# Last output projection's first operands in places of long dead tiles, two stores by GpSimd's queue, splits in pairs, and HGRN's sum in two F32R passes

## The chip, the cores and the metric

The kernel runs on one core of a Trainium2 chip. The metric is the device time of one execution in microseconds; a kernel's time is the median of its runs.

## The reference

One decoder layer on x (1, 2048, 1024) in float32:

```python
h = rmsnorm(x, norm1_w)
proj = h @ w_in                                  # HGRN2 columns | RWKV-7 columns
o_hg = hgrn2(...)                                # 4 heads of 128
o_rw = rwkv7(...)                                # 8 heads of 64
x = x + concat([o_hg, o_rw], -1) @ w_out         # the output projection
x = x + conv_ffn(rmsnorm(x, norm2_w), ...)       # up, causal conv of width 3, silu gate, down; 2816 wide
return rmsnorm(x, final_norm_w)

# the end of hgrn2, per head of 128 channels
o = o * rsqrt(mean(o * o, axis=-1) + 1e-6)
o = o * norm_w * silu(g_raw)
```

## The kernel before

The 2048 tokens are cut into four blocks of 512 (NBLK = 4, BLK = 512). Activations are held with channels on the 128 partitions and tokens in the free dimension.

Large products use no fp32 matmul. Each operand is split into a rounded F32R part and an F32R rest: `hi` is a copy by ACT, `lo` is the difference by DVE (`split_to`, L241 to L243, and `split`, L245 to L251). A product is then three matmuls of 512 columns, hi·hi, hi·lo and lo·hi (`mm3`, L264 to L267), that add up in one PSUM bank.

Phase 1 holds three generators. `dense` issues input projections, and from `out_block` also the output projections of the blocks 0 to 2, into the bank `pj`. `rw_stream` steps through RWKV and `hg_stream` through HGRN. A loop calls one step of each stream and then issues about 2.0 us of dense matmuls by its own count (TICK), so that PE has dense work while a step's other engines are busy. A `yield` is the end of a step.

One `hg_unit` is one head in one block, 16 in all. Its end is what the change touches: the attention output `op` in PSUM is squared by ACT into `osq` (L1044, one step), summed over the 128 channels by a matmul with `ones`, an fp32 matrix of ones (L1047, next step), and turned to a factor by Ln and Exp; DVE multiplies it in, and a DMA stores the result to `oT`. RWKV's sums do the same with `group`, in two passes over a split square (`parts`, then `add_up`, L1057 to L1059).

`out_block(2, ...)` is the last dense work of phase 1. For two halves of its tokens (`i2`) and two halves of the 1024 outputs (`dh`) it multiplies `oT` by `w_out` (tiles `wh`, `wl`, `hh`, `hl`), adds x (`xh`, L408) and stores to `x1d` by SP's queue (L410). RWKV's last value `yo` of the last block is stored to `oT` by GpSimd's queue (L928).

The output projection of block 3 follows in the pool `op`. It runs over dh (2) and over k, the eight groups of 128 channels, in the order 0, 1, 4, 5, 2, 3, 6, 7. Each step loads and splits 128x512 of `w_out` (to `woh`, `wol`) and, for dh = 0, of `oT` (`Bh`, `Bl`, held in `ohl[k]`), and issues twelve matmuls into four banks `wacc`. The first three raw tiles of either kind lie in six places `uraw`, the later ones in `Bh[2]` and `Bl[2]`; they are loaded by SP's queue in the order in which they are written down (L1171). In each of the big tiles `Bh` and `Bl` a list index says which of several places is used.

Where a tile is allocated in a place that an earlier tile held, its first writer waits for the earlier tile's last reader or writer, and also for its stores. The instructions of each engine, and of each DMA queue, go in order; that order is set by a scheduler from the order in the code and its own estimate of times, so an edit of tiles moves instructions.

Of the kernel before, what the change touches and what calls it, by code (L numbers as in the profile page):

```python
# [7 lines left out]
F32 = mybir.dt.float32  # L8
F32R = mybir.dt.float32r
BF16 = mybir.dt.bfloat16  # L10
U32 = mybir.dt.uint32
AF = mybir.ActivationFunctionType
# [6 lines left out]
P = 128  # L19
# [45 lines left out]
def tile_layer(ctx, tc, consts, x, norm1_w, w_in, hg_lb_logits, hg_norm_w, rw_shift_mu, rw_w0, rw_w2,  # L65
# [34 lines left out]
        V.memset(t_, v)  # L100
        return t_

    ones = cp.tile([P, P], F32, name="ones")
    V.memset(ones, 1.0)
    eps6 = eps_tile(1e-6, "eps6")
    epsgn = eps_tile(64e-5, "epsgn")

# [131 lines left out]
        return b11, b22, b12, b21  # L239

    def split_to(hi, lo, src):  # L241
        S.copy(hi, src)
        V.tensor_sub(lo, src, hi.bitcast(F32))  # L243

    def split(pool, src, shape, name, bufs):  # L245

# [16 lines left out]
    def mm3(acc, lhs, rhs, first, last, skip=False):  # L263
        (lh, ll), (rh, rl) = lhs, rhs  # L264
        TE.matmul(acc, lh, rh, start=first, stop=False, skip_group_check=skip)  # L265
        TE.matmul(acc, lh, rl, start=False, stop=False, skip_group_check=skip)  # L266
        TE.matmul(acc, ll, rh, start=False, stop=last, skip_group_check=skip)  # L267

    def phase1(c1):
# [15 lines left out]
        Af = hp.tile([P, 4, P], F32, name="Af")  # L285
        for t_ in (TTs, Af):
            nc.gpsimd.memset(t_, 0.0)
        group = hp.tile([P, P], F32R, name="group")
        hh = hp.tile([P, KD, BLK], F32R, name="hh")
        hl = hp.tile([P, KD, BLK], F32R, name="hl")  # L290

# [82 lines left out]
        def out_block(nb, oh=None, ol=None, then=None):  # L374


            for i2 in range(2):
                for dh in range(2):
                    accs = [bank("pj") for _ in range(2)]
                    for k in range(KD):  # L380
                        if i2 == 0 and dh == 0 and oh is None:
                            raw = stg("sg", "oraw", 2)
                            dma(raw, oT[nb][k * P:(k + 1) * P, :])
                            split_to(hh[:, k, :], hl[:, k, :], raw)
                        if i2 == 1 and dh == 0 and oh is not None:
                            raw = stg("sg", "oraw", 2)[:, 0:256]
                            dma(raw, oT[nb][k * P:(k + 1) * P, 256:512])
                            split_to(hh[:, k, 256:512], hl[:, k, 256:512], raw)
                        raw = wp.tile([P, 512], F32, tag="wraw", name="woraw", bufs=4)
                        wload(raw, w_out[0, k * P:(k + 1) * P, dh * 512:dh * 512 + 512])  # L390
                        wh, wl = split(wp, raw, [P, 512], "w", 4)
                        if k == KD - 2:
                            inputs = dh == 0 and (i2 == 0) == (oh is None)
                            xh = [wp.tile([P, BLK], F32, tag="wraw", name="xh", bufs=4) if inputs else
                                  stg("sg", "xh", 2) for _ in range(2)]
                            for q in range(2):
                                t0 = nb * BLK + (i2 * 2 + q) * P
                                dma(xh[q], x[0, t0:t0 + P, dh * 512:dh * 512 + 512])
                        for q in range(2):
                            is_ = slice((i2 * 2 + q) * P, (i2 * 2 + q + 1) * P)  # L400
                            lhs = ((hh[:, k, is_], hl[:, k, is_]) if oh is None or i2 == 1 else
                                   (oh[k // 4][:, k % 4, is_], ol[k // 4][:, k % 4, is_]))
                            mm3(accs[q], lhs, (wh, wl), k == 0, k == KD - 1)
                            if i2 == 1 and dh == 1 and q == 1:
                                next_block(then, k)
                            yield 680
                    for q in range(2):
                        V.tensor_add(xh[q], accs[q], xh[q])  # L408
                        r0 = (i2 * 2 + q) * P
                        dma(x1d[nb][r0:r0 + P, dh * 512:dh * 512 + 512], xh[q])  # L410

        rows = {}

# [77 lines left out]
        def constants():  # L491

            dma(w2a2[0:64, :], rw_w2[0])
            dma(w2a2[64:128, :], rw_a2[0])
            dma(cst, consts[:, 0:C_ID])
            S.copy(group, blk1)
            dma(g2, rw_g2[0])

        def spread():
# [433 lines left out]
        def hg_unit(nb, j):  # L933
# [108 lines left out]
                TE.matmul(op[:, ts_], SH[:, b, :], q[:, ts_], start=False, stop=True)  # L1042
            sq = rp.tile([P, BLK], F32, tag="hk", name="osq")
            act(sq, op, AF.Square)  # L1044
            yield
            ms = bank("hg")
            TE.matmul(ms, ones, sq, start=True, stop=True)  # L1047
            act(sq, ms, AF.Ln, bias=eps6, scale=1.0 / 128)
            act(sq, sq, AF.Exp, scale=-0.5)
            yield  # L1050
# [68 lines left out]
    with ExitStack() as c2:  # L1119
# [34 lines left out]


        with tc.tile_pool(name="op", bufs=1, reuse_waits="tile") as op_:
            crow = [op_.tile([88, P], F32, name=f"crow{i}") for i in range(2)]
            def rows_of_conv():
                load(crow[0], conv_w[0, 0:2, :].rearrange("w (k p) -> (w k) p", p=P))
                load(crow[1][0:44, :], conv_w[0, 2:3, :].rearrange("w (k p) -> (w k) p", p=P))  # L1160
                load(crow[1][44:88, :], conv_b.rearrange("w (k p) -> (w k) p", p=P))

            b = NBLK - 1
            for _ in range(2):
                pst("skip")
            ohl = {}
            order = [None]

            def load(t_, src):

                i_ = dma(t_, src)  # L1171
                if order[0] is not None:
                    tc.add_manual_dep(i_.ins, order[0].ins.name, NOSYNC, reason="order of loads")
                order[0] = i_

            loader[0] = load
            rings = {"o": (Bh[2], []), "w": (Bl[2], [])}

            def ring(nm, src):

                t_, n_ = rings[nm]
                if len(n_) < 3:
                    v = wr.tile([P, 4, P], F32, tag="uraw", name="uraw", bufs=6).rearrange("p k c -> p (k c)")
                else:
                    v = t_[:, len(n_) % 4, :]
                n_.append(0)
                load(v, src)
                return v

            def take(k):  # L1190

                raw = ring("o", oT[b][k * P:(k + 1) * P, :])
                ohl[k] = tuple(t_[3 + 2 * (k // 4)][:, k % 4, :] for t_ in (Bh, Bl))
                split_to(*ohl[k], raw)

            def weights(k, dh):
                raw = ring("w", w_out[0, k * P:(k + 1) * P, dh * 512:dh * 512 + 512])
                wh, wl = (op_.tile([P, 512], F32R, tag="wo" + c, name="wo" + c, bufs=3) for c in "hl")
                split_to(wh, wl, raw)
                return wh, wl  # L1200

            xt = {}

            def x_tile(i):
                xt[i] = op_.tile([P, 512], F32, tag="xh", name="xh", bufs=8)

            for i in range(4):
                x_tile(i)
            for dh in range(2):
                accs = [pst("wacc") for _ in range(4)]  # L1210
                for n, k in enumerate((0, 1, 4, 5, 2, 3, 6, 7)):
                    w = weights(k, dh)
                    if dh == 0:
                        take(k)
                    if n == 5:
                        for i in range(4):
                            t0 = b * BLK + i * P
                            if dh:
                                x_tile(i)
                            load(xt[i], x[0, t0:t0 + P, dh * 512:dh * 512 + 512])  # L1220
                    if dh == 0 and n == 6:
                        rows_of_conv()
                    if dh == 1 and n == 4:
                        for i, (lo_, hi_) in enumerate(((0, 88), (88, 176))):
                            vps = pst("cps")
                            TE.transpose(vps[:, 0:88], crow[i], ident[0:88, 0:88])
                            V.tensor_copy(cvt[:, lo_:hi_], vps[:, 0:88])
                        A0 = up_raw(0)
                    if dh == 1 and 2 <= n:
                        for j in range(2):  # L1230
                            q = 2 * (n - 2) + j
                            build(0, (0, 1, 4)[q // 4], q % 4)
                    for i in range(4):
                        is_ = slice(i * P, (i + 1) * P)
                        mm3(accs[i], (ohl[k][0][:, is_], ohl[k][1][:, is_]), w, n == 0, n == KD - 1)
                for i in range(4):
                    V.tensor_add(xt[i], accs[i], xt[i])
                    dma(x1d[b][i * P:(i + 1) * P, dh * 512:dh * 512 + 512], xt[i])
# [350 lines left out]
```

## Time and profile before

| | us |
|---|---|
| median of 3 runs | 2686.07 |
| lowest and highest run | 2683.67, 2687.13 |
| the profiled execution's own time | 2685.16 |
| its span in the trace | 2683.4 |
| PE busy in it | 2596.0 |
| DVE busy | 1952.4 |
| ACT busy | 1359.4 |

The mean clock granted to TensorE was 0.992 of full speed. A row of a timeline reads: start in us, busy us, engine, line, operation, output<-inputs, shapes, count of joined instructions, and in brackets the idle time before it with what ended it. Phase 1 ends near 1343 us; the projection of block 3 begins at 1351.01; the last span to 2683 belongs to the ConvFFN.

### The profile page before, as it was taken

To read this page: it belongs to the slowest core of one execution; us is meant where nothing else is said; L and a number is where in the kernel's file an instruction comes from. 1 tells how busy PE (TensorE), PEld (TensorE's weight loads), DVE (VectorE), ACT (ScalarE), POOL (GpSimd) and SP (SyncE) were. 2 spreads that over 40 slices of the span, in tenths; PEclk is the share of its full clock that TensorE was granted. 3 is DMA by queue.
4 is the path that set the end of the run, shared out by engine and by line. 5 is a ranking of instruction groups with operands and counts; after the bars stand their busy time and mean duration, and the time that the engine had idled before them with its cause. 6 is when DMAs were issued, how large, how long until landed. Compare 5 with 4: busy or idle time off the path is not lost.

```text
span 2683.4 us, 47889 instructions
## 1 busy us (share of the span) xinstructions
PE 2596.0 (97%) x18059; PEld 2089.4 (78%) x18059; DVE 1952.4 (73%) x3729; ACT 1359.4 (51%) x2183; POOL 381.7 (14%) x684
## 2 busy tenths in 40 slices
PE   7999999999999999999989999999999999999998
PEld 5877777777777777777778888887888887788887
DVE  4877667576576765767668789988998888676556
ACT  5555453544634545344447665456555545445444
POOL 6433222212322122222100000000000000000000
PEclk9999999999999999999999999999999999999999
DMA  8645443355643556734484458756754463898665
GB/s 302 205 162 169 162 134 123 119 161 200 208 131 119 162 189 200 259 122 131 157 273 146 135 183 264 246 172 206 252 199 146 153 200 122 313 323 281 203 193 185
DMA packets 312830, 510.54 MB, mean 190 GB/s; under 512 B 46879, under 2 KB 143509, under 8 KB 312597
## 3 DMA queue, kind: packets, MB, share of 16 engines
q1 hardware_dynamic: 258225, 329.65, 37.3%
q0 software_dynamic: 54304, 177.80, 20.3%
q8 instruction: 142, 2.33, 0.4%
q14 instruction: 91, 0.75, 0.1%
q10 hardware_dynamic: 68, 0.02, 0.0%
HBM read 373.13 MB, written 134.22 MB: 189 GB/s over the span
## 4 chain that ended last, share of the span: by engine, by line
PE 68%; DVE 10%; DMA 7%; issue 6%; ACT 6%; POOL 1%; SPq 0%; DVEq 0%; POOLq 0%; ACTq 0%
PE pj L265 7%; PE pj L266 7%; PE pj L267 6%; PE ua L265 4%; PE ua L267 4%; PE ua L266 4%; PE da L266 2%; PE da L267 2%; PE da L265 2%; PE ud L266 2%; PE ud L267 2%; PE ud L265 2%; PE hg L979 2%; PE db L267 2%; PE db L265 2%
## 5 line engine op out<-in xcount | busy, mean ns | idle before, releaser
L265 PE MATMUL pj<-hh,wh 128*128 128x512 f32 x960 | 398.0, 415 | 6.2 <-ACT rkv L120 2.9
L266 PE MATMUL pj<-hl,wh 128*128 128x512 f32 x960 | 377.4, 393 | 0.0
L267 PE MATMUL pj<-hh,wl 128*128 128x512 f32 x960 | 377.0, 393 | 0.0
L265 PE MATMUL ua<-Bh,uwh 128*128 128x512 f32 x704 | 276.4, 393 | 3.6 <-ACT m L120 2.5
L267 PE MATMUL ua<-Bh,uwl 128*128 128x512 f32 x704 | 274.3, 390 | 0.0
L266 PE MATMUL ua<-Bl,uwh 128*128 128x512 f32 x704 | 274.1, 389 | 0.0
L265 PEld LDWEIGHTS pj<-hh,wh 128*128 128x128 f32 x960 | 181.0, 189 | 57.9 <-issue 9.0
L267 PEld LDWEIGHTS pj<-hh,wl 128*128 128x128 f32 x960 | 180.9, 188 | 40.0 <-issue 0.6
L266 PEld LDWEIGHTS pj<-hl,wh 128*128 128x128 f32 x960 | 181.3, 189 | 35.9 <-issue 2.6
L249 ACT CAST uwh<-uraw 128x512 fp32r<-128x512 f32 x220 | 134.6, 617 | 129.9 <-PE ua L266 56.2
L250 DVE TENSOR_TENSOR dal<-draw,dah 128x512 fp32r<-128x512 f32 x138 | 95.1, 689 | 111.9 <-ACT dah L249 111.7
L250 DVE TENSOR_TENSOR uwl<-uraw,uwh 128x512 fp32r<-128x512 f32 x220 | 147.1, 684 | 35.2 <-ACT uwh L249 35.2
L249 ACT CAST dah<-draw 128x512 fp32r<-128x512 f32 x138 | 85.8, 622 | 166.1 <-PE da L266 79.6
L265 PEld LDWEIGHTS ua<-Bh,uwh 128*128 128x128 f32 x704 | 132.2, 188 | 34.2 <-ACT m L120 6.0
L267 PEld LDWEIGHTS ua<-Bh,uwl 128*128 128x128 f32 x704 | 132.2, 188 | 28.0 <-DVE uwl L250 0.4
L266 PEld LDWEIGHTS ua<-Bl,uwh 128*128 128x128 f32 x704 | 132.2, 188 | 26.6
L265 PE MATMUL ud<-Bh,uwh 128*128 128x512 f32 x352 | 138.0, 392 | 0.0
L267 PE MATMUL ud<-Bh,uwl 128*128 128x512 f32 x352 | 137.0, 389 | 0.0
L266 PE MATMUL ud<-Bl,uwh 128*128 128x512 f32 x352 | 137.0, 389 | 0.0
L1459 POOL DMA_DIRECT2D gd<-y x2 | 1.1, 555 | 952.3 <-DVE y L1457 952.3
L266 PE MATMUL da<-dbl,dah 128*128 128x512 f32 x332 | 129.5, 390 | 1.0 <-DVE dbl L250 1.0
L267 PE MATMUL da<-dbh,dal 128*128 128x512 f32 x332 | 129.2, 389 | 0.0
(575 smaller groups left out, 6245.0 us busy)
## 6 DMA issues: line engine op xcount, KB each, us to landing
uraw<-in_w_up_dram SPq DMA_DIRECT2D x176, 256.0 KB, 3.3
woraw<-in_w_out_dram POOLq DMA_DIRECT2D x96, 256.0 KB, 3.5
br<-gd SPq DMA_DIRECT2D x88, 256.0 KB, 4.2
draw<-Sg SPq DMA_DIRECT2D x88, 256.0 KB, 3.6
draw<-Tw SPq DMA_DIRECT2D x88, 256.0 KB, 3.4
gd<-y SPq DMA_DIRECT2D x86, 256.0 KB, 2.8
Sg<-br SPq DMA_DIRECT2D x72, 256.0 KB, 2.6
xt<-x1d SPq DMA_DIRECT2D x32, 512.0 KB, 5.9
```

Source lines behind the costliest of these rows:

```text
L249: S.copy(hi, src)
L250: V.tensor_sub(lo, src, hi.bitcast(F32))
L265: TE.matmul(acc, lh, rh, start=first, stop=False, skip_group_check=skip)
L266: TE.matmul(acc, lh, rl, start=False, stop=False, skip_group_check=skip)
L267: TE.matmul(acc, ll, rh, start=False, stop=last, skip_group_check=skip)
L979: TE.matmul(o, kt[:, t0:t0 + 64], qs, start=True, stop=True, tile_position=(0, e * 64))
L1459: (dma if end is None else nc.gpsimd.dma_start)(gd_[2 * h + b][fb * P:(fb + 1) * P, :], ys[0][:, b * BLK:(b + 1) * BLK])
```

## The change

It has six parts.

- The matrix `ones` becomes an F32R tile of the phase's pool, written by ACT (Identity with scale 0 and bias 1 over `blk1`).
- HGRN's squares are split into `hi` and `lo` in the step of the Square, in places of `Sf` and `VT`; two F32R matmuls (`add_up`) replace the fp32 matmul.
- The last two stores of `out_block(2)` (second half of the tokens, dh = 1) go to GpSimd's queue.
- The first pair `woh`, `wol` is allocated at the opening of the pool, ahead of everything else there; the x tiles are allocated when they are loaded. `ohl` uses the places 5 for k < 4 and 3 for k of 4 and more, the other way round than before.
- The splits of the first steps are tied in the order of the code: woh, Bh, woh, Bh on ACT, and wol, Bl, wol, Bl on DVE.
- The first k step issues four hi·hi, then four hi·lo, then four lo·hi, in place of three per row block.

Lines 265 to 267 become 263 to 265, L408 becomes L406, and the matmuls of the last projection have L1247.

```diff
-    ones = cp.tile([P, P], F32, name="ones")
-    V.memset(ones, 1.0)
...
     def split_to(hi, lo, src):
-        S.copy(hi, src)
-        V.tensor_sub(lo, src, hi.bitcast(F32))
+        c_ = S.copy(hi, src)
+        return c_, V.tensor_sub(lo, src, hi.bitcast(F32))
...
-        group = hp.tile([P, P], F32R, name="group")
+        group, ones = (hp.tile([P, P], F32R, name=nm) for nm in ("group", "ones"))
...
-                        dma(x1d[nb][r0:r0 + P, dh * 512:dh * 512 + 512], xh[q])
+                        (nc.gpsimd.dma_start if nb == NBLK - 2 and i2 and dh else dma)(
+                            x1d[nb][r0:r0 + P, dh * 512:dh * 512 + 512], xh[q])
...
             S.copy(group, blk1)
+            act(ones, blk1, AF.Identity, bias=1.0, scale=0.0)
...
             act(sq, op, AF.Square)
+            hi, lo = (rp.tile([P, BLK], F32R, tag=tag, name="part") for tag in ("Sf", "VT"))
+            split_to(hi, lo, sq)
             yield
             ms = bank("hg")
-            TE.matmul(ms, ones, sq, start=True, stop=True)
+            add_up(ms, ones, hi, lo)
...
         with tc.tile_pool(name="op", bufs=1, reuse_waits="tile") as op_:
+            wo_ = {c: [op_.tile([P, 512], F32R, tag="wo" + c, name="wo" + c, bufs=3)] for c in "hl"}
...
+            split_done = []
+
+            def split_next(hi, lo, raw):
+                pair = split_to(hi, lo, raw)
+                if 0 < len(split_done) < 6:
+                    for i_, o_ in zip(pair, split_done[-1]):
+                        tc.add_manual_dep(i_.ins, o_.ins.name, NOSYNC, reason="order of splits")
+                split_done.append(pair)
+
             def take(k):
 
                 raw = ring("o", oT[b][k * P:(k + 1) * P, :])
-                ohl[k] = tuple(t_[3 + 2 * (k // 4)][:, k % 4, :] for t_ in (Bh, Bl))
-                split_to(*ohl[k], raw)
+                ohl[k] = tuple(t_[5 - 2 * (k // 4)][:, k % 4, :] for t_ in (Bh, Bl))
+                split_next(*ohl[k], raw)
 
             def weights(k, dh):
                 raw = ring("w", w_out[0, k * P:(k + 1) * P, dh * 512:dh * 512 + 512])
-                wh, wl = (op_.tile([P, 512], F32R, tag="wo" + c, name="wo" + c, bufs=3) for c in "hl")
-                split_to(wh, wl, raw)
+                wh, wl = (wo_[c].pop() if wo_[c] else
+                          op_.tile([P, 512], F32R, tag="wo" + c, name="wo" + c, bufs=3) for c in "hl")
+                split_next(wh, wl, raw)
                 return wh, wl
...
-            for i in range(4):
-                x_tile(i)
...
-                            if dh:
-                                x_tile(i)
+                            x_tile(i)
                             load(xt[i], x[0, t0:t0 + P, dh * 512:dh * 512 + 512])
...
-                    for i in range(4):
-                        is_ = slice(i * P, (i + 1) * P)
-                        mm3(accs[i], (ohl[k][0][:, is_], ohl[k][1][:, is_]), w, n == 0, n == KD - 1)
+                    terms = [(ohl[k][0], w[0]), (ohl[k][0], w[1]), (ohl[k][1], w[0])]
+                    first = n == 0 and dh == 0
+                    for q in range(12):
+                        i, t_ = (q % 4, q // 4) if first else (q // 3, q % 3)
+                        TE.matmul(accs[i], terms[t_][0][:, i * P:(i + 1) * P], terms[t_][1],
+                                  start=n == 0 and t_ == 0, stop=n == KD - 1 and t_ == 2)
```

The order of instructions, ACT at the end of phase 1 and the start of the last projection, before: `wh` are the last weights of `out_block(2)`, `yo` is RWKV's last value, `woh` and `Bh` belong to the last projection, and the number behind a name tells one place from another.

```order
L249 CAST wh<-woraw 128x512 x2
L120 ACTIVATE yo<-yo,vt 128x512 x2
L116 ACT_TABLE_LOAD
L242 CAST woh<-uraw 128x512 x3
L242 CAST Bh_14735<-uraw 128x512 x2
L242 CAST Bh_14738<-uraw 128x512
L242 CAST Bh_14738<-Bh_14730 128x512
```

The same place now.

```order
L247 CAST wh<-woraw 128x512 x2
L118 ACTIVATE yo<-yo,vt 128x512 x2
L247 CAST wh<-woraw 128x512 x2
L114 ACT_TABLE_LOAD
L240 CAST woh<-uraw 128x512
L240 CAST Bh_14818<-uraw 128x512
L240 CAST woh<-uraw 128x512
L240 CAST Bh_14818<-uraw 128x512
L240 CAST woh<-uraw 128x512
L240 CAST Bh_14815<-uraw 128x512
```

The casts of woh and Bh alternate, and two casts of `wh` moved behind those of `yo`.

DVE at the same place, before: `wl` are the rests of the weights of `out_block(2)`, L927 writes `yo`, L408 adds x.

```order
L1052 TENSOR_TENSOR osq<-osq,hgg 128x512
L926 TENSOR_TENSOR yo<-yo,BV 128x1024
L250 TENSOR_TENSOR wl<-woraw,wh 128x512
L927 TENSOR_TENSOR yo<-rw,yo 128x1024
L408 TENSOR_TENSOR xh<-pj,xh 128x512 x2
L243 TENSOR_TENSOR wol<-uraw,woh 128x512 x3
L243 TENSOR_TENSOR Bl_14736<-uraw,Bh_14735 128x512 x2
L243 TENSOR_TENSOR Bl_14739<-uraw,Bh_14738 128x512
```

And now.

```order
L1054 TENSOR_TENSOR osq<-osq,hgg 128x512
L926 TENSOR_TENSOR yo<-yo,BV 128x1024
L248 TENSOR_TENSOR wl<-woraw,wh 128x512
L927 TENSOR_TENSOR yo<-rw,yo 128x1024
L248 TENSOR_TENSOR wl<-woraw,wh 128x512 x2
L406 TENSOR_TENSOR xh<-pj,xh 128x512 x2
L241 TENSOR_TENSOR wol<-uraw,woh 128x512
L241 TENSOR_TENSOR Bl_14819<-uraw,Bh_14818 128x512
L241 TENSOR_TENSOR wol<-uraw,woh 128x512
L241 TENSOR_TENSOR Bl_14819<-uraw,Bh_14818 128x512
L241 TENSOR_TENSOR wol<-uraw,woh 128x512
L241 TENSOR_TENSOR Bl_14816<-uraw,Bh_14815 128x512
```

Two subtractions `wl` now stand behind L927, where none stood, and wol and Bl alternate; the Bl of the third pair (place 14816) is the one for k = 4.

PE at the first k step of the projection, before.

```order
L267 MATMUL pj<-wh,hl 128x512
L265 MATMUL wacc<-woh,Bh_14735 128x512
L266 MATMUL wacc<-wol,Bh_14735 128x512
L267 MATMUL wacc<-woh,Bl_14736 128x512
L265 MATMUL wacc<-woh,Bh_14735 128x512
L266 MATMUL wacc<-wol,Bh_14735 128x512
```

And now.

```order
L265 MATMUL pj<-wh,hl 128x512
L1247 MATMUL wacc<-woh,Bh_14818 128x512 x4
L1247 MATMUL wacc<-wol,Bh_14818 128x512 x4
L1247 MATMUL wacc<-woh,Bl_14819 128x512 x4
L1247 MATMUL wacc<-woh,Bh_14818 128x512
L1247 MATMUL wacc<-wol,Bh_14818 128x512
```

The first four matmuls need woh and Bh alone; wol is read by the fifth, where it was by the second, and Bl by the ninth, where it was by the third.

## The prediction

> **What bounds the kernel now.** I read the page's busy times first, then the chain of waits, then windows around the edit, then the timeline of each engine there.
>
> ```profile
> PE 2596.0 (97%) x18059; PEld 2089.4 (78%) x18059; DVE 1952.4 (73%) x3729; ACT 1359.4 (51%) x2183; POOL 381.7 (14%) x684
> PE 68%; DVE 10%; DMA 7%; issue 6%; ACT 6%; POOL 1%; SPq 0%; DVEq 0%; POOLq 0%; ACTq 0%
> 25.00:1300.00 1275.00, 1233.57 (x11970) 972.21 (x11968) 859.29 (x2048) 615.14 (x976) 344.07 (x614) 0.99 0.52 168
> 1300.00:1343.00 43.00, 38.40 (x267) 29.44 (x264) 26.10 (x54) 19.89 (x34) 5.92 (x11) 0.92 0.55 177
> 1343.00:1356.00 13.00, 5.12 (x13) 3.73 (x13) 5.87 (x10) 4.26 (x8) 0.72 (x1) 0.61 0.91 312
> 1356.00:1368.00 12.00, 12.00 (x54) 9.91 (x53) 4.78 (x8) 4.67 (x8) 0.00 (x0) 1.00 0.41 136
> 1368.00:1416.00 48.00, 46.60 (x205) 37.59 (x204) 38.72 (x67) 28.54 (x49) 0.00 (x0) 1.00 0.94 312
> ```
>
> TensorE is busy 97% of the span, so time is won in two ways only: fewer microseconds of matmul, or a hole closed. After the span, the columns of a window are the busy times of PE, weight load, DVE, ACT and POOL, then granted clock, DMA share and GB/s. The worst hole is 1343 to 1356, between the mixers and the last output projection: PE works 5.12 of 13 us, at a clock of 0.61. From 1356 to 1368 PE is full and the DMA engines are half idle (0.41); from 1368 to 1416 they are nearly full (0.94).
>
> The timelines of PE, ACT, DVE and SP show how the hole arises, with two pieces of the chain of waits:
>
> ```profile
> 1342.73 0.40 PE L267 MATMUL pj<-wh,hl 128*128 128x512 f32 x1
> 1351.01 0.80 PE L265 MATMUL wacc<-woh,Bh 128*128 128x512 f32 x1 [7.88 <-ACT Bh L242]
> 1352.58 0.63 PE L265 MATMUL wacc<-woh,Bh 128*128 128x512 f32 x1
> 1353.00 0.63 PE L266 MATMUL wacc<-wol,Bh 128*128 128x512 f32 x1
> 1356.03 0.40 PE L265 MATMUL wacc<-woh,Bh 128*128 128x512 f32 x1
> 1356.26 0.39 PE L266 MATMUL wacc<-wol,Bh 128*128 128x512 f32 x1
> 1339.80 1.28 ACT L116 ACT_TABLE_LOAD   x1
> 1348.78 1.66 ACT L242 CAST woh<-uraw 128x512 fp32r<-128x512 f32 x3 [7.70 <-DMA oT<-yo]
> 1350.35 1.66 ACT L242 CAST Bh<-uraw 128x512 fp32r<-128x512 f32 x3
> 1340.96 0.68 DVE L250 TENSOR_TENSOR wl<-woraw,wh 128x512 fp32r<-128x512 f32 x1
> 1341.56 1.22 DVE L927 TENSOR_TENSOR yo<-rw,yo 128x1024 f32<-128x1024 f32 x1
> 1342.69 1.28 DVE L408 TENSOR_TENSOR xh<-pj,xh 128x512 f32<-128x512 f32 x2
> 1325.95 18.36 SPq L410 DMA_DIRECT2D x1d<-xh  x4
> 1344.36 0.46 SPq L1171 DMA_DIRECT2D Bl<-in_w_out_dram  x1
> 1341.56 1.23 DVE yo L927
> 1343.34 5.34 DMA oT<-yo
> ```
>
> The last matmul of the mixers starts at 1342.73. The first of the projection wants Bh. ACT was free at 1341.1 (the table load's end), yet did the three woh casts at 1348.78 and Bh behind them: their tiles stand where `yo` stood, and `yo` is released by its store, 5.34 us long. So the hole is a wait for a place; the first operands had been loaded long before. When PE resumes it goes at a pitch of 0.42 us (1352.58 to 1353.00), not 0.23 (1356.03 to 1356.26). The first k step, 12 matmuls, takes 1351.01 to 1356.03 = 5.02 us where 12 x 0.23 = 2.7 would do.
>
> **The change part by part.** *The HGRN sum* (16 units). Rows of the PE timeline, fp32 sum of HGRN, then the two-pass sums RWKV uses; then the groups:
>
> ```profile
> 138.25 1.02 PE L1047 MATMUL hg<-osq,ones 128*128 128x512 f32 x2
> 138.70 0.79 PE L265 MATMUL pj<-hh,wh 128*128 128x512 f32 x1
> 139.33 0.39 PE L266 MATMUL pj<-hl,wh 128*128 128x512 f32 x1
> 1331.62 0.39 PE L1058 MATMUL rw<-part,group 128*128 128x512 f32 x1
> 1332.08 0.39 PE L1058 MATMUL rw<-part,group 128*128 128x512 f32 x1
> 136.37 0.60 ACT L120 ACTIVATE osq<-hg 128x512 f32<-128x512 f32 x1 [3.36 <-PE hg L1042]
> L1059 PE MATMUL rw<-part,group 128*128 128x512 f32 x48 | 20.1, 419 | 3.1 <-DVE part L243 3.1
> L1058 PE MATMUL rw<-part,group 128*128 128x512 f32 x48 | 20.0, 416 | 1.5 <-ACT part L242 1.5
> L1047 PE MATMUL hg<-osq,ones 128*128 128x512 f32 x32 | 16.5, 596 | 0.0
> L243 DVE TENSOR_TENSOR part<-yo,part 128x1024 fp32r<-128x1024 f32 x8 | 9.8, 1222 | 13.3 <-ACT part L242 13.3
> ```
>
> The fp32 pair pushes the next matmuls back until 139.33; less one pj pitch of 0.23 it costs 139.33 - 0.23 - 138.25 = 0.85 us. Two F32R passes cost 1332.08 - 1331.62 = 0.46. Saved: 0.39 x 16 = 6.2 us of PE.
>
> Against it stand one cast and one subtraction per unit, and PE now waits for them. A cast costs a third of the woh group, 0.55 us; a subtraction 0.68 alone (the wl row), 0.60 in a queue (1341.56 - 1340.96). From the Square's start the second pass needs 0.60 + 0.55 + 0.60 = 1.75 us, the first 1.15. In the row shown the sum came 138.25 - 136.37 = 1.88 us after the Square's start, filled with dense matmuls. That covers it by 0.13 us, if neither ACT nor DVE is busy elsewhere; DVE is so 859.29/1275 = 67% of this stretch. The nearest price is RWKV's: its splits are twice as wide (a subtraction 1.22), its two passes are laid out alike, and the groups show 3.1 + 1.5 = 4.6 us of waits over 24 pairs of sums, 0.19 each. Bounds: 0 (fully covered, as L1047 is now) to the whole added 1.15 us per unit, 0 to 18.4. I take RWKV's 0.19 x 16 = 3.0, because shape and order are its own. The 8.8 us of added casts and 9.6 of subtractions lie on engines with room, and cost nothing besides while PE has matmuls queued. Net -3.2, from -6.2 to +12.2. `ones` by ACT is one instruction at the start, beside loads: 0.
>
> *The hole.* In the new order woh and Bh follow the table load with no wait, because the first pair sits in a place long dead. They take 1341.1 + 2 x 0.55 = 1342.2 for the first pair: ready before PE. But on DVE the last two wl subtractions now stand behind L927, where the old order had one before it. L927 ends 1342.8; two subtractions of 0.60 end 1344.0; the last dense matmuls for them end about 1345.2, 2.1 later than before (1342.73 + 0.4). The first four hi-hi matmuls run 1345.2 to 1346.1, without wol. DVE first does the two xh additions, which end 1.28 us after the last matmul at 1346.5, less what the first of them does early; wol stands behind them. I put wol at 1346.7, Bl 0.6 later, and the end of the first twelve at 1348.5: 12 x 0.23 from 1345.2 plus 0.6 of wait. Before, they ended at 1356.03. Gain 7.5 us. The x loads only change places in SP's queue: 0.
>
> The slow pitch followed a wait of 7.88 us; after the wait below, of 1.94 us, it was 0.33 and then 0.24:
>
> ```profile
> 1322.53 0.50 PE L265 MATMUL pj<-wh,hh 128*128 128x512 f32 x1 [1.94 <-ACT hh L242]
> 1322.86 0.40 PE L266 MATMUL pj<-wl,hh 128*128 128x512 f32 x1
> 1323.10 0.40 PE L265 MATMUL pj<-wh,hh 128*128 128x512 f32 x1
> ```
>
> So I expect no slow stretch after the shorter gaps that remain. If the gaps join into a long one, ten matmuls at the slow pitch return (0.42 - 0.23) x 10 = 1.9 us. The Trainium skill, "TensorE: Matmul & The Clock Gate", section "Part 1: The HAM clock gate", puts half clock behind an idle window of about 3.4 us, for about as long. By that rule the sum is the same; the trace agrees at 7.88 and at 1.94 us, and no row here lies between.
>
> *The stores by GpSimd.* Its queue is no longer SP's, but SP's next load still waits for the last dense matmul, so SP begins at about 1345.4, not 1344.36: a debt of 1 us. The new wait is DVE's: Bl of the third step (k = 4) now waits for GpSimd's store to land, and all later subtractions queue behind it, with PE behind them. Rows of the DMA view:
>
> ```profile
> oT<-osq SPq DMA_DIRECT2D x12, 256.0 KB, 2.2
> oT<-osq POOLq DMA_DIRECT2D x4, 256.0 KB, 3.2
> x1d<-xh SPq DMA_DIRECT2D x32, 256.0 KB, 4.0
> ```
>
> The same store takes 1.0 us longer by GpSimd. Issued at about 1346.5 it lands 3.2 to 5.0 later (SP's 4.0 plus that 1.0), 1349.7 to 1351.5; PE wants it after two steps, 1348.5 + 2.7 = 1351.2. Cost 0 to 0.9 (0.6 of it the subtraction), taken as 0.3. The Trainium skill, "DMA: Bandwidth & Descriptors", section on SWDGE and HWDGE, speaks against this edit: descriptors that GpSimd builds in software are set up more slowly than SP's, and DVE can hold up their writing. The two oT rows agree, with 3.2 against 2.2 us; were DVE to hold the store for both xh additions, 1.28 us, the sum would be 2678.4.
>
> *The debt of the transfers.* Between 1343 and 1416 the DMA engines now move what they need at 0.91, 0.41 and 0.94 of their time: 11.8 + 4.9 + 45.1 = 62 of 73 us. If PE asks 7.5 us sooner, 62 of 65 must be used. I take 1.7 us returned, from the 1.4 us (48.00 - 46.60) that PE already loses there; bounds 0 and 7.5. The hole's net: -7.5 + 0.3 + 1.7 = -5.5, from -7.5 to 0.
>
> Sum: 2685.16 - 3.2 - 5.5 = 2676.5 on the profiled execution, whose span is 2683.4; the median of the runs is 0.9 higher, 2686.07, so **2677.4**.
>
> **The rivals.** *Both gains whole:* splits covered everywhere, transfers with room. 2686.07 - 6.2 - 7.5 = 2672.4. For it: L1047's 0.0 of waits and the room of 1356 to 1368.
>
> *Transfers decide the stretch:* the hole closes and opens again before 1416, so of 7.5 only about 1 stays. 2686.07 - 3.2 - 1 = 2681.9. For it: 0.94 share over 48 us. Against: 41% in the 12 us before, which can be filled.
>
> *A late GpSimd store or a half-clock stretch:* 1.9 more is given back, 2679.3. For it: DMA share 0.91 just then.
>
> *The splits stall PE (slower):* ACT and DVE take each cast and subtraction in their queue's order, behind work up to 1.22 us long, and PE stands in order behind the sum. With w of wait per unit the sum is 16 (w - 0.39) - 5.5: it is zero at w = 0.73, and over 0.2% slower (5.4 us, about the least that a measurement can tell from no change) at w = 1.07. Uncovered whole, 1.15 each: +12.2 - 5.5 = +6.7, 2692.8. For it: a cover of 1.88 against 1.75. Against: RWKV's 0.19 with wider splits.
>
> **How the numbers follow.** Forecast 0.50, both gains whole 0.10, late store or half clock 0.12: faster by over 0.2% in all, 0.72. Transfers decide: 0.17, within 0.2%. Splits stall: 0.11, slower. The range must leave out at most 2 in 10: 2668 (4 below the best case, for holes closed elsewhere in 25 to 1300, where PE idles 41 us) to 2685, past the transfers' case and as far as a wait of 0.66 us per unit, 16 x (0.66 - 0.39) - 5.5 = -1.2.
>
> **What would show it.** Right: the two-pass sum shows under 4 us of waits over 32 rows; the first wacc starts by about 1345 to 1346 with an idle of under 2 us, at a pitch of 0.23; the first twelve wacc matmuls end near 1348.5, not 1356.03. Wrong: the sum's group shows over 12 us of waits on part; Bl's third subtraction waits for x1d by over 1 us; or ua's first matmuls begin at the old distance, with new waits on `br` or `uraw`.

## The result and the profile after

Over nine runs of each the changed kernel has a median of 2674.75 us (2670.84 to 2680.74), the kernel before 2683.74 us (2680.22 to 2687.15). The ratio is 0.9967, interval 0.9955 to 0.9978: 9.0 us faster, where 8.7 were forecast. The profiled execution is one of the longer ones, 2680.46 us with a span of 2678.7, so its trace shows 4.7 us less than that of before; what goes with that is at the end.

The first row of the page of after, and the windows that were shown of before (busy PE, weight load, DVE, ACT, POOL, granted clock, DMA share, GB/s):

```profile
PE 2595.9 (97%) x18059; PEld 2089.1 (78%) x18059; DVE 1964.4 (73%) x3744; ACT 1368.4 (51%) x2200; POOL 383.2 (14%) x686
25.00:1300.00 1275.00, 1231.37 (x11922) 971.45 (x11920) 867.69 (x2060) 622.07 (x989) 344.33 (x614) 0.99 0.52 168
1300.00:1343.00 43.00, 38.19 (x304) 28.08 (x302) 27.59 (x56) 23.18 (x40) 6.01 (x12) 1.00 0.57 184
1343.00:1356.00 13.00, 11.86 (x48) 8.96 (x49) 7.84 (x13) 4.67 (x9) 1.74 (x3) 1.00 0.81 281
1356.00:1368.00 12.00, 12.00 (x54) 9.87 (x54) 6.14 (x10) 4.85 (x10) 0.00 (x0) 1.00 0.81 279
1368.00:1416.00 48.00, 45.98 (x202) 37.08 (x201) 40.30 (x71) 31.07 (x55) 0.00 (x0) 1.00 0.91 300
```

The hole is closed: from 1343 to 1356 PE now works 11.86 of 13 us at full clock, and the DMA engines have 0.81 of their time taken from 1356 to 1368, where it was 0.41. DVE and ACT have 12.0 and 9.0 us more to do than before, close to the 9.6 and 8.8 of the added splits.

The timelines of PE, ACT and DVE of after at the same place:

```profile
1345.17 0.39 PE L265 MATMUL pj<-wh,hl 128*128 128x512 f32 x1
1345.40 1.08 PE L1247 MATMUL wacc<-woh,Bh 128*128 128x512 f32 x4
1346.94 1.21 PE L1247 MATMUL wacc<-wol,Bh 128*128 128x512 f32 x4 [0.46 <-DVE wol L241]
1347.99 1.09 PE L1247 MATMUL wacc<-woh,Bl 128*128 128x512 f32 x4
1348.92 0.39 PE L1247 MATMUL wacc<-woh,Bh 128*128 128x512 f32 x1
1340.40 1.28 ACT L114 ACT_TABLE_LOAD   x1
1341.69 0.62 ACT L240 CAST woh<-uraw 128x512 fp32r<-128x512 f32 x1
1342.22 0.62 ACT L240 CAST Bh<-uraw 128x512 fp32r<-128x512 f32 x1
1341.12 1.22 DVE L927 TENSOR_TENSOR yo<-rw,yo 128x1024 f32<-128x1024 f32 x1
1342.26 1.28 DVE L248 TENSOR_TENSOR wl<-woraw,wh 128x512 fp32r<-128x512 f32 x2
1344.92 1.37 DVE L406 TENSOR_TENSOR xh<-pj,xh 128x512 f32<-128x512 f32 x2 [1.38 <-PE pj L265]
1346.20 0.68 DVE L241 TENSOR_TENSOR wol<-uraw,woh 128x512 fp32r<-128x512 f32 x1
```

woh and Bh follow the table load with no wait and are ready 2.6 us before PE wants them. The dense matmuls end later than before, because the two wl subtractions stand behind L927. PE waits once, 0.46 us, for wol behind the two additions of x, and the first k step ends at 1348.92. The prediction had 1345.2, 0.6 and 1348.5.

HGRN's sum in the groups of after, with RWKV's:

```profile
L1060 PE MATMUL hg<-part,ones 128*128 128x512 f32 x16 | 7.9, 491 | 0.0
L1061 PE MATMUL hg<-part,ones 128*128 128x512 f32 x16 | 7.1, 446 | 0.0
L1061 PE MATMUL rw<-part,group 128*128 128x512 f32 x48 | 20.5, 427 | 3.6 <-DVE part L241 3.6
L1060 PE MATMUL rw<-part,group 128*128 128x512 f32 x48 | 20.0, 417 | 1.7 <-ACT part L240 1.7
```

PE never waited for HGRN's parts. The 3.0 us of waits that were taken over from RWKV are not there; RWKV's own went from 4.6 to 5.3.

### The profile page after: what moved, and what is told of

Same layout as the page of the kernel before. It is cut to its first block, busy times and chain, and to the rows that moved or that the text cites. A ratio compares the mean times of both kernels' runs of the same rounds, so it can differ in the third digit from the quotient of the medians.

```text
span 2678.7 us, 47929 instructions
## 1 busy us (share of the span) xinstructions
PE 2595.9 (97%) x18059; PEld 2089.1 (78%) x18059; DVE 1964.4 (73%) x3744; ACT 1368.4 (51%) x2200; POOL 383.2 (14%) x686
```

## The experiments

Single profiles of one kernel differ by several microseconds, so the kernels are laid side by side by four marks of their profiles: the start of yo's last product (L927 in after), the start of the last dense matmul, the end of the first k step (the start of the thirteenth wacc matmul), and the span. The last column is the time, ahead of yo's last product, that the clock's records in the trace give to TensorE at half clock. It differs between two profiles of one kernel too (after and change_again), and it moves the first mark.

| kernel | yo's last product | last dense matmul | first k step ends | span | us at half clock before yo's |
|---|---|---|---|---|---|
| before | 1341.56 | 1342.73 | 1356.03 | 2683.4 | 27.3 |
| after | 1341.12 | 1345.17 | 1348.92 | 2678.7 | 23.9 |
| change_again | 1332.82 | 1336.88 | 1340.63 | 2669.7 | 10.2 |
| hgrn_only | 1331.99 | 1336.03 | 1344.09 | 2669.4 | 10.2 |
| hgrn_rests_first | 1334.06 | 1335.37 | 1346.88 | 2670.5 | 10.2 |
| hole_only | 1339.48 | 1340.66 | 1344.49 | 2675.2 | 27.3 |
| places_undone | 1333.23 | 1337.27 | 1344.62 | 2671.2 | 23.9 |
| pairs_undone | 1334.30 | 1338.35 | 1342.96 | 2671.3 | 17.1 |
| first_step_undone | 1340.41 | 1344.49 | 1349.28 | 2676.4 | 27.3 |
| sp_stores | 1336.75 | 1340.80 | 1344.52 | 2671.9 | 23.9 |
| rests_first | 1334.02 | 1335.31 | 1339.04 | 2668.3 | 20.5 |
| splits_fp32_sum | 1332.29 | 1334.98 | 1338.81 | 2669.5 | 10.2 |
| sum_three_times | 1347.63 | 1348.81 | 1352.64 | 2683.8 | 30.7 |

**hgrn_only.** HGRN's part on the kernel before (three dots stand for lines left out).

```diff
...
+            hi, lo = (rp.tile([P, BLK], F32R, tag=tag, name="part") for tag in ("Sf", "VT"))
+            split_to(hi, lo, sq)
...
-            TE.matmul(ms, ones, sq, start=True, stop=True)
+            add_up(ms, ones, hi, lo)
```

> Only HGRN's sum is changed (ones in F32R, split squares, two passes); the last projection is as before. My theory: 6.2 us of TensorE time saved, about 3 of them lost again in waits, so 3.2 us below before (ratio 0.9988). Rival A: the added 18 us of casts and subtractions delay ACT and DVE work that TensorE waits for (RWKV's M, ZT and part), and the saving is lost whole: 0, ratio 1.000 (0.9995 to 1.001). Rival B: nothing is lost: 6.2 below, 0.9977. The hole in front of the last projection stays, with an idle of 6 to 8 us, since woh still waits for the store of yo.

Measured: 2671.63 us against 2681.91, ratio 0.9962 (0.9950 to 0.9974), 10 us faster. That is a miss: all three readings left the hole as it was, and none came to 10. The timelines of PE and ACT, the piece of the chain of waits with yo's store, and SP's first load:

```profile
1339.29 0.50 PE L263 MATMUL wacc<-woh,Bh 128*128 128x512 f32 x1 [2.88 <-ACT Bh L240]
1337.06 1.66 ACT L240 CAST woh<-uraw 128x512 fp32r<-128x512 f32 x3 [4.52 <-DMA oT<-yo]
1333.77 3.19 DMA oT<-yo
1337.53 0.45 SPq L1172 DMA_DIRECT2D Bl<-in_w_out_dram  x1
```

woh still waits for the store of yo, but the hole is 2.88 us instead of 7.88. Two things were found here. The two wl subtractions behind yo's last product come with HGRN's part, not with the projection's: hole_only lacks them. (The scheduler's order is touchy: sum_three_times has none behind it, and splits_fp32_sum one.) They keep 2.9 us of dense matmuls back (the last one starts 4.04 us behind yo's last product, 1.17 in before), and these now run while yo is stored. And the store itself takes 3.19 us, not 5.34. So not all of the 5.0 us is won: from yo's last product to the end of the first k step it is 12.10 us here and 14.47 in before, 2.4 less.

**hgrn_rests_first** turns that order back in hgrn_only: the last wl subtractions ahead of yo's last addition and product.

```diff
...
-            V.tensor_add(y2, y2, BV)
+            a_ = V.tensor_add(y2, y2, BV)
+            if nb == NBLK - 1 and s_ == 1:
+                last_yo[0] = a_
...
+                        if last_yo[0] is not None:
+                            tc.add_manual_dep(last_yo[0].ins, last_sub[0].ins.name, NOSYNC, reason="rests first")
```

> HGRN's sum alone, with the last three subtractions wl put ahead of the last two products of yo. My theory of hgrn_only: about 5 of its 10 us come from the two subtractions that moved behind yo, since the dense matmuls then fill the time of yo's store (idle 2.88 us, not 7.88) and SP's loads, which wait for the last of them, no longer share the store's transfer (3.2 us, not 5.3). With the order turned back the hole opens again: idle of 6 to 8 us ahead of the first wacc, and the time is 4 to 6 us above hgrn_only, ratio about 0.998. Rival: the gain is all phase 1's, and the time stays within 1.5 us of hgrn_only.

Measured: 0.9981 (0.9970 to 0.9992), 2675.13 us: 3.5 us above hgrn_only by the medians, 5.1 by the ratios, each with its own runs of before. PE, the store, and SP's queue:

```profile
1342.51 0.79 PE L265 MATMUL wacc<-woh,Bh 128*128 128x512 f32 x1 [6.76 <-ACT Bh L240]
1335.86 5.37 DMA oT<-yo
1335.91 0.92 SPq L412 DMA_DIRECT2D x1d<-xh  x2
1336.88 0.45 SPq L1178 DMA_DIRECT2D Bl<-in_w_out_dram  x1
```

The hole is open again at 6.76 us, and the store takes 5.37: SP's two stores and its first loads start within 1.1 us of it. In hgrn_only the loads start 3.8 us behind it (1337.53). So of the 3.9 us by which the two holes differ, 2.2 are the longer store, which runs beside SP's transfers here and in before (5.34, loads 1.0 us behind), and alone in hgrn_only. That SP's transfers lengthen it is read from these three profiles; it was not tried by itself.

**hole_only.** The change with the fp32 sum.

```diff
...
-            hi, lo = (rp.tile([P, BLK], F32R, tag=tag, name="part") for tag in ("Sf", "VT"))
-            split_to(hi, lo, sq)
...
-            add_up(ms, ones, hi, lo)
+            TE.matmul(ms, ones, sq, start=True, stop=True)
```

> The change without HGRN's part: places, pairs, first k step and GpSimd stores, with the fp32 sum. DVE's order ahead of the last projection is then that of before (no wl subtraction behind the last product of yo), so the last dense matmul should end at about 1343, the first k step at about 1346.6: 9.4 us earlier than before, less 1.5 us of transfers: 8 below (ratio 0.9970). If the two subtractions moved behind yo are no consequence of HGRN's part, the step ends 7.1 earlier, and the time is 5.5 below (0.9980).

Measured: 0.9970 (0.9958 to 0.9982), 8.2 us faster, as expected of the first theory. The first k step ends 3.83 us behind the last dense matmul, 13.30 in before. DVE and PE in the third step:

```profile
1348.35 0.69 DVE L243 TENSOR_TENSOR Bl<-uraw,Bh 128x512 fp32r<-128x512 f32 x1 [3.45 <-DMA x1d<-xh]
1349.09 0.50 PE L1246 MATMUL wacc<-woh,Bl 128*128 128x512 f32 x1 [1.27 <-DVE Bl L243]
```

This is the wait that the prediction named: DVE's third Bl waits for GpSimd's store, and PE 1.27 us behind it. In change_again DVE waited 1.33 us there, and PE not at all.

**places_undone.** The change with woh, wol, the x tiles and ohl in their old places.

```diff
...
-            wo_ = {c: [op_.tile([P, 512], F32R, tag="wo" + c, name="wo" + c, bufs=3)] for c in "hl"}
...
+            for i in range(4):
+                x_tile(i)
...
```

> The whole change, but woh, wol, the x tiles and ohl in the places of before. If the wait for a place is the hole's cause, woh waits for the store of yo again (idle of PE about 3 to 4 us after the last dense matmul at 1345, since the store lands at 1348.5), with a first k step that ends 4 to 7 us later than in the change: the time is 4 to 7 above the change, ratio to before 0.998 to 1.000. Rival (order of splits or of matmuls is what counts): within 1 us of the change, 0.9967.

Measured: 0.9975 (0.9960 to 0.9989), 0.8 in a thousand (2 us) above the change's first measurement and level with its second. That is a miss: 4 to 7 us were expected, and by time the two are not told apart. The profile tells them apart. ACT's row, then PE's:

```profile
1338.30 0.62 ACT L240 CAST woh<-uraw 128x512 fp32r<-128x512 f32 x1 [4.52 <-DMA oT<-yo]
1339.49 1.20 PE L1248 MATMUL wacc<-woh,Bh 128*128 128x512 f32 x4 [1.84 <-ACT Bh L240]
1343.59 1.20 PE L1248 MATMUL wacc<-woh,Bl 128*128 128x512 f32 x4 [1.98 <-DVE Bl L241]
```

woh waits for yo's store again, and Bl as well, so the step ends 7.35 us behind the last dense matmul where the change has 3.75. The places are worth 3.6 us at that point. Behind it 2.5 of them are gone: from the end of the step to the end of the span it is 1326.6 us here and 1329.1 in change_again.

**pairs_undone.** The tie between the splits is taken out (its condition never holds).

```diff
-                if 0 < len(split_done) < 6:
+                if 0 > len(split_done):
```

> The whole change without the order of the splits: three casts of woh, then Bh; three subtractions wol, then Bl. ACT ends Bh at about 1343.8, still before TensorE wants it (1345.4). On DVE the first Bl ends 1.2 us later, at 1348.6, where its first matmul was at 1348.0: 0.6 us above the change (ratio to before 0.997). Rival: pairs are what closes the hole: 3 us or more above the change.

Measured: 0.9963 (0.9950 to 0.9976), within the change's interval. The first k step ends 4.61 us behind the last dense matmul, 0.86 later than in the change. The rival of 3 us falls.

**first_step_undone.**

```diff
-                    first = n == 0 and dh == 0
+                    first = False
```

> The whole change, but the first k step goes row block by row block (hi hi, hi lo, lo hi) as before. The second matmul then needs wol, which ends about 1.5 us after the last dense matmul, and the third Bl, 0.6 later; nine follow at 0.23, so the step ends about 0.7 us later than in the change: 0.7 above it, less than the runs can tell; the profile decides, by the distance from the last dense matmul's start to the step's end (3.75 us in the change, 4.4 here). Rival: none of it is left, if Bl is the last operand anyway and the other eight matmuls wait behind it.

Measured: 0.9971 (0.9958 to 0.9984). The step ends at 1349.28, 4.79 us behind the last dense matmul, 1.04 more than in the change:

```profile
1346.27 0.51 PE L1247 MATMUL wacc<-wol,Bh 128*128 128x512 f32 x1 [1.15 <-DVE wol L241]
1346.87 0.50 PE L1247 MATMUL wacc<-woh,Bl 128*128 128x512 f32 x1
```

The second matmul waits 1.15 us for wol, where the change has three more to issue first and waits 0.46. Pairs and order are worth about 1 us each at the step, and nothing that the times can show.

**sp_stores.**

```diff
-                        (nc.gpsimd.dma_start if nb == NBLK - 2 and i2 and dh else dma)(
+                        dma(
```

> The whole change, but all stores to x1d by SP's queue. In the change and its relatives DVE's third Bl waited 1.2 to 3.5 us for GpSimd's store. With SP that store lands about 1 us sooner, but SP's first load of the last projection stands behind two stores that wait for the additions, and starts about 1 us later. My theory: the two cancel, within 1 us of the change (0.9971 over two measurements). Rival: SP's queue is the bound after the hole, 1.5 to 2 us above.

Measured: 0.9971 (0.9959 to 0.9983): no difference. DVE's third Bl no longer waits for a store, and SP's first load starts 1.51 us behind the last dense matmul instead of 0.42 (1345.59 in after). The two cancel, as far as the runs can tell.

**places_alone.** The places on the kernel before, nothing else.

```diff
...
+            wo_ = {c: [op_.tile([P, 512], F32R, tag="wo" + c, name="wo" + c, bufs=3)] for c in "hl"}
...
-                ohl[k] = tuple(t_[3 + 2 * (k // 4)][:, k % 4, :] for t_ in (Bh, Bl))
+                ohl[k] = tuple(t_[5 - 2 * (k // 4)][:, k % 4, :] for t_ in (Bh, Bl))
...
-            for i in range(4):
-                x_tile(i)
...
```

> Of the change only the places: first pair woh and wol, the x tiles and ohl; everything else as before (fp32 sum, stores by SP, splits and first k step in the old order). If the places are the hole's cause, the casts follow the table load with no wait. Three woh, then Bh: Bh is ready 3 x 0.52 + 0.62 after the table load, at about the last dense matmul; wol three times ahead of the first Bl. The first k step then ends about 1 us later after the last dense matmul than in hole_only, and the ratio is 0.997 to 0.9975. Rival: without pairs and the new first step the hole stays half open, 4 us above hole_only, 0.9985.

Measured: 0.9986 (0.9975 to 0.9998), 4 us faster over twelve runs: nearer to the rival. Its profiled execution, a thirteenth, took 2875.18 us at a granted clock of 0.85, so no time of its trace is used, and how much of the hole stayed open is not settled.

**change_again.** The changed kernel a second time.

> The changed kernel itself, beside the others on one chip. My theory holds that single profiles of the same phase 1 differ by about 4 us either way, through stretches at half clock of 3.4 us each that come and go; then this one is within 1.5 us of the first measurement: ratio 0.9967 (0.9955 to 0.998), with another set of slow stretches. Rival: the sums of the parts (hgrn_only 10 below, hole_only 8 below) should add up somewhere, so that it is 3 us or more below hgrn_only.

Measured: 0.9975 (0.9965 to 0.9986), 7.0 us faster. Both measurements hold the forecast. The span of its profile is 9.0 us shorter than that of after, and 8.3 of these lie ahead of yo's last product, in the same instructions, with 13.7 us less of half clock there. The rival falls: it is 1.9 us above hgrn_only by the medians (3.5 by the ratios, each with its own runs of before), not 3 below.

**splits_fp32_sum.** The change with its splits, but the sum by the fp32 matmul.

```diff
-            add_up(ms, ones, hi, lo)
+            TE.matmul(ms, ones.bitcast(F32), sq, start=True, stop=True)
```

> The whole change with the squares split as in it, but summed by the fp32 matmul from the unsplit square; the parts are not read. It has the load of the splits without the saving: if the 6.2 us of TensorE time are real and reach the end, it is 6 us above change_again. Rival: other waits fill what is saved, and it is within 2 us of change_again.

Measured: 0.9965 (0.9953 to 0.9977). The group of its sum is as dear as before:

```profile
L1049 PE MATMUL hg<-osq,ones 128*128 128x512 f32 x32 | 16.5, 596 | 0.0
```

Yet it is not slower than change_again, and 6 us above it lies outside the intervals. My theory falls here. Its profile and that of change_again have the same time at half clock, so they can be compared up to yo's last product. First change_again, then splits_fp32_sum, the window with PE's busy time in front, and the wait of PE (25 to 1340; us in total, times, longest) that differs most:

```profile
25.00:1332.82 1307.82, 1260.80 (x12211) 993.96 (x12209) 892.60 (x2114) 642.30 (x1026) 348.89 (x625) 1.00 0.51 170
PE rw L857 <- ACT M L118: 10.9, 7, 3.0
25.00:1332.29 1307.29, 1265.15 (x12216) 995.20 (x12214) 892.70 (x2114) 642.55 (x1026) 349.49 (x625) 1.00 0.51 170
PE rw L857 <- ACT M L118: 5.0, 7, 1.8
```

With the fp32 sum PE is busy 4.4 us longer and idle 4.9 us shorter (42.1 against 47.0), and it arrives 0.5 us earlier. So in this pair of profiles the rival holds: the time that the two-pass sum frees is spent waiting, mostly for RWKV's M.

**sum_three_times.**

```diff
-            add_up(ms, ones, hi, lo)
+            for _ in range(3):
+                add_up(ms, ones, hi, lo)
```

> The whole change, with HGRN's two-pass sum issued three times over (each time from the start, so the result is the same): 4 more matmuls of 0.23 us in each of 16 units, 14.7 us more of TensorE time. splits_fp32_sum has 6.2 us more than the change and was not slower. If TensorE's time is the bound of phase 1, this is 15 us above the change, ratio 1.002 to 1.003. If the chains through ACT and DVE set the pace there and the matmuls only fill their waits, it is within 4 us, 0.997 to 0.9985. I hold with a case between, 5 to 10 us above, since the waits of phase 1 (40 us) can swallow about 5.

Measured: 1.0027 (1.0015 to 1.0039), 7.8 us slower than before, and 0.0056 or 15 us above sp_stores and first_step_undone, which were measured beside it (0.9971 both). That is the first of the two cases, not the one between that I held with: added TensorE time does lengthen the kernel. But not all 15 us need be matmuls. The mean granted clock of its runs is 0.9935, and 0.9954 and 0.9956 in the other two, which by itself could be up to 5 us.

**rests_first.** The change with the order of hgrn_rests_first.

> The whole change, with the last three subtractions wl put ahead of the last two products of yo. Nothing waits for yo's store in the change, so the order that suits the dense matmuls is free: the last of them should end at about 2 us earlier against yo's products, and the first k step with it, at an idle under 1 us. 1.5 to 2 us below change_again. Rivals: the later store of yo holds SP's x loads and the later k steps, or the full DMA engines take it back: 0; noise of the slow stretches hides it.

Measured: 0.9969 (0.9957 to 0.9981), 1.4 us below change_again by the medians, less than the intervals. Its last dense matmul starts 1.29 us behind yo's last product instead of 4.06, as meant, but yo's products now stand behind three subtractions. It is not shown to beat the change, and no kernel here is.

## Why the prediction was right, and where its parts were not

The total was right, 8.7 forecast and 9.0 and 7.0 measured. That the sum came out so well is in part luck: hole_only alone is 8.2 us faster, where the hole's net was forecast at 5.5, and HGRN's 3.2 beside it are not seen. The parts, by the marks:

**HGRN's sum, forecast -3.2.** The waits were mis-sized: 3.0 us were taken over from RWKV's row, and HGRN's sum shows 0.0. L1047's own 0.0 was nearer, since the cover of 1.88 us was enough for a chain of 1.75. So the prediction's sum should have come to -6.2. What the runs show is not that either. In the whole change the sum earns nothing that they can tell: six kernels with the projection part and the two-pass sum (after, change_again, pairs_undone, first_step_undone, sp_stores, rests_first) have ratios of 0.9963 to 0.9975, mean 0.9969, and the two with the fp32 sum have 0.9970 (hole_only) and 0.9965 (splits_fp32_sum). The marks agree where the time at half clock is the same. At 27.3 us yo's last product starts at 1341.56 and 1339.48 with the fp32 sum and at 1340.41 with two passes; at 10.2 us it starts at 1332.29 with the fp32 sum and at 1331.99, 1332.82 and 1334.06 with two passes. The step of the prediction that failed is that a microsecond of TensorE saved in phase 1 comes off its end: in the pair of profiles under splits_fp32_sum some 5 us of waits stand in its place, as many as I had allowed for in sum_three_times, whose 14.7 added us are more than that. Why hgrn_rests_first, with the hole still open, is 5.1 us faster than before (interval 2.1 to 8.0) is not settled; its first k step accounts for 1.8 (11.51 against 13.30 us behind the last dense matmul).

**The hole, forecast -7.5.** From the last dense matmul to the end of the first k step: 13.30 us before, 3.75 in after and in change_again, so -9.55. The last dense matmul itself is later by 4.05 - 1.17 = 2.9 against yo's last product. Net -6.7; the replay from rows of before was right to 0.8 us, all of it in how late the last dense matmul comes (2.1 forecast). The wait for a place is shown as its cause by places_undone and hgrn_only, where woh waits for the store of yo by name. In time the places alone give 4 us (places_alone, 0.5 to 6.7), and the whole projection part 8.2 (hole_only).

**The debt of the transfers, forecast 1.7, with 0.3 for GpSimd's store.** From the first k step's end to the span's end it is 1327.4 us in before, 1329.8 in after, 1329.1 in change_again: 2.4 and 1.7 given back (after has 3.4 us of half clock at 1856 that the other two lack, up to 1.7 of its 2.4). Against the kernels of this study in which the hole stays open wholly or in part it is more: 1325.3 in hgrn_only, 1323.6 in hgrn_rests_first, 1326.6 in places_undone, and with before 1325.7 in the mean. The nine that end the step within 4.8 us of the last dense matmul have 1327.1 to 1331.2, mean 1329.3. So some 3.6 us are returned. This is one reason why hgrn_only and hole_only, 10 and 8 us alone, are 7 to 9 together; the other is that hgrn_only already has 5.2 of the 9.55 us by which the step comes closer to the last dense matmul. Rows of change_again show part of the debt, two of ACT, one of PE, and two of the waits of PE between 1334 and 1440:

```profile
1376.86 1.27 ACT L240 CAST Bh<-br 128x512 fp32r<-128x512 f32 x2 [4.52 <-DMA br<-h2d]
1378.25 0.62 ACT L240 CAST woh<-Bl 128x512 fp32r<-128x512 f32 x1
1378.92 0.49 PE L1247 MATMUL wacc<-woh,Bh 128*128 128x512 f32 x1 [1.16 <-ACT woh L240]
PE wacc L1247 <- ACT woh L240: 1.6, 2, 1.2
PE ua L263 <- ACT uwh L247: 1.0, 1, 1.0
```

ACT waits 4.52 us for a load, woh stands behind it in ACT's order, and PE waits 1.16 us for woh; before has no wait of wacc behind its first step. The operands of the later steps are asked for sooner than they come. The prediction's mechanism is seen here, and its 2.0 us hold against before; against all the kernels with an open hole they are about half.

**The rivals.** Splits that stall PE: HGRN's sum has no waits on part, so it never came near its 0.73 us per unit. Both gains whole: the sum of -6.2 and -7.5 was not reached, because of the debt and because the 6.2 did not arrive. Transfers that decide the stretch: they took some 2 to 4 of 9.5 us, not all but one. A late GpSimd store: seen, DVE waits 1.33 to 3.52 us for it in six profiles, and PE behind it 1.33 in sum_three_times, 1.27 in hole_only, 0.58 in rests_first, 0.21 in splits_fp32_sum and nothing in change_again and pairs_undone. A half-clock stretch: none at the first step in after and change_again. Of the signs of being right all came: no waits on the two-pass sum, wacc with no idle at 1345.40 and at a pitch of 0.23, the step's end at 1348.92. But one of the signs of being wrong came too: Bl's third subtraction waits for x1d by over 1 us (1.33 in change_again; the 1.22 in after the profile puts down to a cast). It cost PE nothing there, so it was a poor sign.

What it did not see is that the two parts touch: HGRN's splits moved DVE's order at the end of phase 1, and hgrn_rests_first shows that this took 3.9 of the 5.0 us out of the hole, in part by moving matmuls into it.

## What to carry to other kernels

A wait in front of a stage may be a wait for a place and not for data: look at which store ends it, and whether the first operands can stand in tiles that died long ago. Two edits that shorten the same stretch don't add, above all where its transfers are near full; measure each alone and both together. And in a kernel whose order a scheduler makes, an edit's effect on the order at a place far from it can be as large as its own. Before two single profiles are compared, see that they have the same time at half clock.

## What the runs showed of the hardware

The same gap can cost half the clock or nothing. In two executions of the changed kernel PE waits at the same place for the same subtraction, and then issues the same matmuls. After first, with two later matmuls of the stretch and two windows (PE's busy time in front, the granted clock third from the end), then change_again:

```profile
650.27 0.50 PE L264 MATMUL pj<-wl,hh 128*128 128x512 f32 x1 [1.92 <-DVE wl L248]
652.49 0.63 PE L264 MATMUL pj<-wl,hh 128*128 128x512 f32 x1
652.91 0.63 PE L265 MATMUL pj<-wh,hl 128*128 128x512 f32 x1
647.48:650.89 3.41, 1.49 (x7) 0.91 (x6) 3.41 (x7) 2.97 (x4) 0.00 (x0) 1.00 0.51 199
650.89:654.30 3.41, 3.41 (x10) 2.64 (x9) 2.60 (x4) 1.52 (x3) 0.00 (x0) 0.50 0.09 34
```

```profile
650.14 0.50 PE L264 MATMUL pj<-wl,hh 128*128 128x512 f32 x1 [1.94 <-DVE wl L248]
651.63 0.39 PE L264 MATMUL pj<-wl,hh 128*128 128x512 f32 x1
651.86 0.39 PE L265 MATMUL pj<-wh,hl 128*128 128x512 f32 x1
645.63:649.05 3.42, 2.40 (x10) 1.36 (x8) 3.42 (x6) 3.40 (x7) 0.00 (x0) 1.00 0.30 116
649.05:652.46 3.41, 2.32 (x10) 1.84 (x11) 3.41 (x6) 2.51 (x3) 0.00 (x0) 1.00 0.47 182
```

After 1.92 us of idle time the pitch is 0.42 us in the one and 0.23 in the other, with the granted clock at 0.50 and 1.00. The prediction read 1.94 us as short enough. It need not be, and before itself shows it: from 1308.07 to 1311.05 its matmuls go at a pitch of 0.42, behind gaps of 0.63, 0.50 and 1.29 us.

What differs is where a grid cuts the gap. In each of the thirteen traces of the table the granted clock changes only at whole multiples of 3.41 us from its other changes, and the windows above are cut on that grid. In after the whole gap falls into one window, PE is busy 1.49 of its 3.41 us, and half clock follows; in change_again the grid divides the gap, PE is busy 2.40 and 2.32 us, and none follows. Cutting all thirteen traces so (without their first 40 and last 30 us), every one of the 43 full-clock windows in which PE was busy under 0.445 of the time was followed by half clock, 26 of the 328 between that and 0.775, and none of the 9449 above. These shares are of PE's rows, whose ends are modelled; what decides between 0.445 and 0.775 is not known. The Trainium skill, "TensorE: Matmul & The Clock Gate", section "Part 1: The HAM clock gate", says that the window of activity runs freely, so that where a matmul falls in it varies; the two executions agree. It gives an idle window of about 3.4 us as the cause of half clock; here 1.92 us was enough.

These stretches go with the spread of the runs. The profile of after has seven windows of 20 us ahead of 1240 with a clock under 0.97, the one of change_again two, and their spans differ by 9.0 us. Of sp_stores the three shortest runs, 2666 to 2668 us, have a mean clock of 0.997 or 0.998, the longest, 2682.84, has 0.992. A kernel moves them too: the mean over the runs of before is 0.9924 to 0.9930 in three sets, that of the changed kernel 0.9958 and 0.9953. The hole of before has 10.24 us of half clock, 0.0019 of this difference of about 0.003.
